# A hybrid decoder layer: SBUF places, mix, key, query and V-row transfers of the attention stage rearranged

## The chip, the cores and the metric

One Trainium2 chip, one core, float32. The metric is the device time of one execution in microseconds (us), the median of the runs. The engines are TensorE (PE, with its weight loads as PEld), VectorE (DVE), ScalarE (ACT), GpSimd (POOL) and SyncE (SP). Every engine works through its own instructions in order. DMA transfers are issued by SP, ACT and POOL, each of which has a queue of its own.

## What is computed

One layer for a prompt of 4096 tokens and for 64 sample tokens (8 sequences of 8), width 1024:

```python
h = _rmsnorm(x, g_pre)
z = h @ w_in                      # 1024 -> 2816 columns, split into
cb, cc, ch, cg, q, k, v, ag, mq, mg = _split_cols(z)
out_a = silu(cg) * cb * conv3(cc * ch)                    # 256 columns
out_b = silu(ag) * window_attention(q, k, v, sink)        # 512 columns, window 128, 8 heads on 2 kv heads
out_c = silu(mg) * cross_attention(mq, mem_k, mem_v)      # 256 columns, 256 memory tokens, 4 heads
y = concatenate([out_a, out_b, out_c]) @ w_out            # 1024 -> 1024
return x + _rmsnorm(y, g_post)
```

The keys and values of the window and of the memory and the ends of the convolution are returned as well.

## The kernel before

**Two stages.** The input projection runs in three phases over 8 blocks of 520 tokens each; phases 1 and 2 make every product from seven partial products (a Strassen scheme, `PRODUCTS`), and a step is one such product `p` of one block `b`. Phase 2 (`ph == 2`) projects six column tiles, the queries 10, 11 and 18 to 21. Its 56 steps are counted by `n = 7 * (b - 1) + p`, and `third_jobs` places other work into them: the keys and values of the memory, the turning of V into rows (`v_load`, `v_turn`), and the scores and weights of the first three attention groups (`EARLY`, `PIECES`). Results go to DRAM: `qd` (keys and queries, a high and a low part), `vd` and `vn` (V as columns and as rows), `md` (the gates, called mix).

The attention stage then runs over 32 blocks of 128 tokens (`blocks`, `Block.run`); in the course of block `i`, `events_of(i, block)` calls for the work on other groups at fixed places `(p, k)` between the matmuls of the output projection (half `p` of the columns, row tile `k`; line 1617 in the profile). In block `i` group `i + 3` gets its scores (`scores`: band scores `ws`, cross scores `xs`), group `i + 1` its values (`values`: products `pv`, then the gate on DVE, lines 1336 and 1367, which multiplies into the mix), and block `i + 1` is split for the output projection (`split`, `mh` and `ml`). A chunk is two groups: 256 tokens, whose keys `kst` (384 KB), queries `q` (two halves of 768 KB) and mix (1 MB) are loaded together for the two.

**The way of a group's weights.** After the softmax (`s`) DVE turns the weights in blocks of 32 x 32 (`turn(0, g)`, `turn(1, g)`; lines 1303 and 1307), 16 transfers of 64 KB move them to `w` (line 1312; by SP, for the first three groups by POOL), POOL masks the bands (`turn(2, g)`, line 1322, four instructions into `wd` and `w`), and then the values of the group can be multiplied.

**Order.** From the start of phase 2 on, the order on each engine is the order in which the code is written. `store` appends its transfer to a list `late` that `flush` sends to SP's queue at the start of a step and after every product. SP's transfers before the steady blocks are: the `qd` stores of the projection's last rows, `blocks[0].load()` and `blocks[1].load()` (`xr`, 512 KB each), the 16 of `w3`, the output `o_yp` of block 0, a V row tile `vh`, the next `xr`, the 16 of `w4`.

**Places.** SBUF places are stacks of pools, and the attention stage opens its pools (`open_attention`) where those of the projection ended. A tile waits until the pools that its own pool overlaps have had their last use. In bytes per partition, counted from the first place behind `place`:

| Phase 2 | before | after the change |
|---|---|---|
| `hx` (x tiles; at the end raw rows of `w_out`) | 0 to 16640 | the same |
| `hp` (high and low parts of x) | 16640 to 33280 | the same |
| `t2` (temporary tiles; at the end the high parts of six rows) | 33280 to 45760 | the same |
| `z8` / `z9` | 45760 / 49920 | 45760 / 52000 |
| `y0` / `y1` | 54080 / 56160 | 49920 / 56160 |
| `z10` / `y2` (to 64480) | 58240 / 62400 | the same |

In the last block of phase 2, the rows of the first half lie in `z9` and `y1`, those of the second in `z10` and `y2`; `z8` and `y0` were last used by the block before.

| Attention stage | before | on | after the change | on |
|---|---|---|---|---|
| `yq` (products times gain) | 0 | `hx` | 0 | `hx` |
| `kp` (keys of even chunks) | 28928 | `hp` | 4096 | `hx` |
| `mixp` (mix of odd chunks) | 8448 | `hx` | 7168 | `hx` |
| `bq` (queries of even chunks) | 16640 | `hp` | 16640 | `hp` |
| `sp` (scores of even groups from 4) | 32000 | `hp`, `t2` | 45760 | `z8`, `y0`, `z9` |
| `wl` (turned weights of odd groups from 3) | 40192 | `t2`, `z8` | 53952 | `z9`, `y1`, `z10` |
| `yp` (two `xr`) | 48384 | `z8`, `z9`, `y0`, `y1` | 35072 | `t2` |
| `wd0`, `wd1` (masked halves) | 4096, 6144 | `hx` | 43264, 62144 | `t2`; `z10`, `y2` |
| `sm`, `bp` (sample) | 56576, 57344 | `y1`; `y1`, `z10`, `y2` | 15360, 28928 | `hx`; `hp`, `t2` |

The mix of even chunks lies in `place`, the queries and keys of odd chunks and the weights of even groups elsewhere; these do not move.

Of the kernel before, what the change touches and what calls it, by code (L numbers as in the profile page):

```python
# [8 lines left out]
F32 = mybir.dt.float32  # L9
# [6 lines left out]
P = 128  # L16
# [4 lines left out]
NS = 64  # L21
# [5 lines left out]
NCH = 4096 // CT  # L27
# [24 lines left out]
def hybrid_layer(ctx: ExitStack, tc: tile.TileContext, a: dict):  # L52
    nc = tc.nc
    DMA = nc.sync
# [67 lines left out]
    def z_pool(where, name, w=2):  # L122
        return where.enter_context(tc.tile_pool(name=name, bufs=1))

    def open_phase(ph):
        nonlocal tp, natp, pa2, pa1

        if ph == 0:
            z = [z_pool(kept_z, f"z{n}") for n in range(4)]
            natp = own.enter_context(tc.tile_pool(name="nat", bufs=2))  # L130
            zp[2] = [*z, z_pool(own, "z4")]
            kept_z.z4 = zp[2][-1]
        elif ph == 1:
            zp[2].remove(kept_z.z4)
            zp[2][:0] = [z_pool(own, f"z{n}") for n in (5, 6, 7)]
        else:
            tp = own.enter_context(tc.tile_pool(name="t2", bufs=6))
            z = [z_pool(own, n) for n in ("z8", "z9", "y0", "y1", "z10", "y2")]
            zp[2], zp[1] = [z[0], z[1], z[4]], [z[2], z[3], z[5]]
        if ph < 2:  # L140
            tp = own.enter_context(tc.tile_pool(name=f"t{ph}", bufs=(7, 9)[ph]))
        bank = lambda where, name, bufs=1: where.enter_context(tc.tile_pool(name=name, bufs=bufs, space=bass.MemoryType.PSUM))
        if ph == 0:
            pa2 = {(tag, 0): bank(psa, f"p{tag}2") for tag in "yx"} | {(tag, 1): bank(own_banks, f"p{tag}3") for tag in "yx"}
        elif ph == 2:
            own_banks.close()
            third["ps"] = bank(psa, "psm", 2)
            pa1 = {("y", 2): pa2["y", 0], ("x", 2): pa2["x", 0], ("x", 1): bank(psa, "px1"), ("y", 1): bank(psa, "py1")}
# [22 lines left out]
            zp[w] += [used[w][i] for i in order if i < len(used[w])]  # L171
            used[w] = []

    late = []

    def flush():
        for fn in late:
            fn()
        late.clear()

    store_queue = [G]

    def store(dst, src):
        if store_queue[0] is G:
            G.dma_start(dst, src)
        else:
            late.append(lambda: DMA.dma_start(dst, src))
# [554 lines left out]
    third = {}  # L742
# [120 lines left out]
    def open_group(g):  # L863
# [6 lines left out]
              (4, 0, of("early_cross_exps")), (4, 1, of("band_weights")), (5, 0, of("early_cross_weights")), (5, 0, of("turn_band")),  # L870
              (6, 0, of("turn_cross")))
    PIECES = {0: (*STAGES, (9, 0, of("masks")), (15, 0, of("values"))), 1: (*STAGES, (9, 0, of("masks")), (15, 0, of("values"))),
              2: (*STAGES, (11, 2, of("masks")))}

    def v_load(k):
        third["v", k] = t = temp(f"vl{k}")[:, :512]
# [2 lines left out]
    def v_turn(k):  # L879

        turned = temp(f"vq{k}")[:, :512]
        V.transpose(turned, third.pop(("v", k)))
        rows_of = vn[512 * k : 512 * k + 512, :].rearrange("(b i) d -> i b d", i=32)
        for g in range(4):
            ds = slice(32 * g, 32 * g + 32)
            store(rows_of[:, :, ds], turned[ds].rearrange("p (b j) -> p b j", j=32))

    def first_chunk():

# [74 lines left out]
    def input_projection():  # L964
        for i, (ph, b, p) in enumerate(steps):
# [39 lines left out]
                slots[0].append(gpost_load)  # L1005
            if ph == 2 and b == last:
                for n, j in enumerate(((), (), (), (0, 1, 2, 3), (4, 5, 6, 7), (8, 9, 10, 11), (12, 13, 14, 15))[p]):
                    slots[(0, 0, 2, 2)[n] if p == 6 else (0, 1, 1, 2)[n]].append(lambda j=j: wo_split(j))
                for j in ((), (0, 2, 4), (6, 8), (), (10, 12, 14), (), ())[p]:
                    slots[2].append(lambda j=j: wo_load(j))  # L1010
                if p == 6:
                    slots[0].insert(0, blocks[0].split)
# [45 lines left out]
    def open_attention():  # L1058

        nonlocal ps, mixp, wp, wl, kp, bp, bq, yp, yq, sp  # L1060
        own.close()
        psa.close()
        pa.close()

        ps = {tag: ctx.enter_context(tc.tile_pool(name=f"ps{tag}", bufs=1, space=bass.MemoryType.PSUM)) for tag in (*range(4), "pv", 4, 5)}
        left = lambda name, bufs=1: att.enter_context(tc.tile_pool(name=name, bufs=bufs))
        yq, wd0, wd1 = left("yq"), left("wd0"), left("wd1")
        left("gap").tile([P, NS], F32, name="gap")
        mixp, bq, kp, sp, wl, yp = left("mixp"), left("bq"), left("kp"), left("sp"), left("wl"), left("yp", 2)
        wp = wd0, wd1  # L1070
        third["sm"], bp = left("sm"), left("bp")

    ps = mixp = wp = wl = vp = kp = bp = bq = yp = yq = sp = None
    att = ctx.enter_context(ExitStack())
# [36 lines left out]
    class Chunk:  # L1111
# [25 lines left out]
        def load_mix(self):  # L1137

            if self.c % 2 == 0:
                self.mix = place.rearrange("p a k n -> p (a k n)")[:, : KT * CT].rearrange("p (k n) -> p k n", k=KT)  # L1140
            else:
                self.mix = mixp.tile([P, KT, CT], F32, tag="mix", name=f"mix{self.c}")
            (G if 0 < self.c < 3 else DMA).dma_start(self.mix, md[:, :, self.ts].rearrange("k p n -> p k n"))

        def early_values(self):

# [16 lines left out]
    class Group:  # L1163
# [32 lines left out]
        def scores(self):  # L1196
            self.open_scores()
            bands = [psum(n, f"ws{self.b}_{n}").rearrange("p (h k) -> p h k", h=2) for n in ((1, 2, 5, 4) if self.b == 4 else range(4))]
            cross_bank = lambda hh: psum(hh if self.b == 4 else 4 + hh, f"xs{self.b}_{hh}").rearrange("p (j k) -> p j k", j=2)
            if self.b != 4:  # L1200
                cross = [cross_bank(hh) for hh in range(2)]
            self.bands(bands[:2], 0)
            tail(0)
            self.bands(bands[2:], 1)
            if self.b == 4:
                cross = [cross_bank(hh) for hh in range(2)]
            self.crosses(cross)
            if self.b == 4:
                turn(1, 3)
            loads = query_loads((self.b - 3) // 2 + 3) if self.b % 2 and self.b > 3 else ()  # L1210
            for fn in loads[:2]:
                fn()
            tail(1)
            for fn in loads[2:]:
                fn()
            if self.b == 3:
                blocks[1].split(0)
            self.band_softmax()
            return cross
# [190 lines left out]
    def query_loads(c):  # L1410
        if c >= NCH:
            return ()
        chunks[c] = Chunk(c)
        return [chunks[c].load_keys, lambda: chunks[c].load_queries(0), lambda: chunks[c].load_queries(1)]

    def chunk_load(c):
# [257 lines left out]
    def events_of(i, block):  # L1674
# [3 lines left out]
        def at(p, k, fn, *args):  # L1678
            ev.setdefault((p, k), []).append(lambda: fn(*args))
# [11 lines left out]
        if i == 30:  # L1691
            at(0, 5, blocks[32].split)
            at(1, 1, blocks[31].split)
            at(1, 6, blocks[31].load)
        if i % 2 == 0:
            if i == 28:
                at(0, 3, lambda: chunks[15].load_mix())
        elif 1 < i and (i + 3) // 2 < NCH - 1:
            at(0, 3, lambda: chunks[(i + 3) // 2].load_mix())
        at(1, 1, turn, 2, i + 2)  # L1700
        if i == 0:
            at(1, 1, chunk_load, 3)
        if i == 1:
            at(1, 1, lambda: chunks[2].load_mix())
        if i > 0 and i + 3 < 2 * NCH:
            at(0, 5, half_load, i + 3)
        if i > 1:
# [126 lines left out]
```

## Time and profile before

| | |
|---|---|
| median of 3 runs | 1494.75 us (1494.41 to 1496.84) |
| profiled execution | 1492.81 us, its span 1491.1 us |
| granted TensorE clock, mean | 0.996 |
| PE / DVE / ACT / POOL busy | 1463.1 / 1212.2 / 758.0 / 457.5 us |
| phase 2, first to last product | 668.22 to 942.05 us |
| output projection starts | 942.05 us |
| moved by DMA | 337.27 MB, mean 226 GB/s |

The span counts from the first to the last instruction; the time has the start and the end of the execution around it. In a row of the timeline stand: start, duration (us), engine, line, operation, tiles written <- tiles read, count, and in square brackets how long the engine had idled before and what it waited for. Tile names in the profile are without their number: `s` is any of `s3`, `s4`. Where rows of one instruction follow each other they are merged, and the duration is that of all.

### The profile page before, as it was taken

Reading aid. Unit: us, or ns where it says so; the run is one execution under the profiler, and the core shown is the slowest. Engines: PE = TensorE matmul, PEld = TensorE weight load, DVE = VectorE, ACT = ScalarE, POOL = GpSimd, SP = SyncE. Lnnn points to the kernel's source line nnn. Section 1 sums busy time; section 2 is a strip of 40 time slices with the busy share of each in tenths; the row PEclk is TensorE's granted clock in tenths of the full one; section 3 lists DMA queues with packets and bytes.
Section 4 is the critical chain, followed back from the end, with each engine's and each line's share of the span. In section 5 each row is a group of like instructions: output and inputs, shape, how many; then the busy total and the mean of one; then the engine's idle time right before and its main releaser. Section 6 shows DMA issues by size and latency. Waiting matters only on the chain.

```text
span 1491.1 us, 30884 instructions
## 1 busy us (share of the span) xinstructions
PE 1463.1 (98%) x11459; PEld 1339.4 (90%) x11459; DVE 1212.2 (81%) x1889; ACT 758.0 (51%) x1869; POOL 457.5 (31%) x633
## 2 busy tenths in 40 slices
PE   9999999999999999999999999889999999999998
PEld 9999999999999999999999999767777777777766
DVE  6779888898998877797667877878988888898853
ACT  6776566466422222244544454555655655565542
POOL 0223332212300000000002225445566465565551
PEclk9999999999999999999999999999999999999999
DMA  9989999887854333258978989998999998989672
GB/s 256 193 244 229 289 289 275 230 272 247 233 208 161 133 117 130 104 211 242 323 258 238 310 260 301 312 209 204 226 242 223 236 240 209 212 220 243 202 218 100
DMA packets 211068, 337.27 MB, mean 226 GB/s; under 512 B 55269, under 2 KB 124773, under 8 KB 210885
## 3 DMA queue, kind: packets, MB, share of 16 engines
q1 hardware_dynamic: 157429, 223.80, 51.1%
q0 software_dynamic: 44416, 79.73, 21.6%
q10 hardware_dynamic: 9072, 31.77, 6.9%
q8 instruction: 91, 1.49, 0.5%
q14 instruction: 60, 0.49, 0.1%
HBM read 192.48 MB, written 110.15 MB: 203 GB/s over the span
## 4 chain that ended last, share of the span: by engine, by line
PE 69%; DMA 13%; DVE 7%; issue 5%; SPq 4%; ACT 2%; POOL 1%; ACTq 0%; DVEq 0%; POOLq 0%
PE c L381 46%; PE y L1617 15%; DMA w<-s 4%; PE pv L1097 4%; SPq L1312 3%; PE ws L1097 1%; DMA qd<-z 1%; DMA mix<-md 1%; DMA place<-md 1%; DVE z L388 1%; DMA wor<-in_w_out 1%; DMA xr<-in_x_p 1%; PE mem_acc L809 1%; DMA o_yp<-xr 1%; PE xs L1097 1%
## 5 line engine op out<-in xcount | busy, mean ns | idle before, releaser
L1617 PE MATMUL y<-wo,mh 128*128 128x512 f32 (+1 forms) x1040 | 328.6, 391 | 0.0
L388 DVE TENSOR_TENSOR z<-c,z 128x520 f32<-128x520 f32 (+1 forms) x308 | 193.7, 643 | 79.0 <-PE c L381 72.6
L1617 PEld LDWEIGHTS y<-wo,mh 128*128 128x128 f32 x1040 | 194.2, 188 | 52.5 <-DVE wmx L1255 5.4
L1617 PE MATMUL y<-wo,ml 128*128 128x512 f32 (+1 forms) x520 | 201.1, 387 | 0.0
L1295 POOL TENSOR_SCALAR s<-s,xrd 128x256 f32<-128x256 f32 x128 | 60.8, 489 | 209.2 <-DVE xrd L1292 163.0
L1617 PEld LDWEIGHTS y<-wo,ml 128*128 128x128 f32 x520 | 97.8, 188 | 18.7 <-DVE ml L1592 0.2
L1265 ACT ACTIVATE s<-s,wnm 128x128 f32<-128x128 f32 x256 | 98.7, 387 | 0.0
L1242 ACT COPY s<-ws 128x256 f32<-128x256 f32 x128 | 41.1, 378 | 90.9 <-PE ws L1097 65.2
L754 POOL MEMSET negs<- 128x1 f32 x1 | 0.1, 98 | 267.2 <-PE c L381 267.2
L1647 POOL TENSOR_TENSOR xr<-yn,xr 128x1024 f32<-128x1024 f32 x31 | 74.4, 2399 | 24.2 <-ACT yn L1646 24.0
L1625 ACT ACTIVATE y<-y 128x512 f32<-128x512 f32 (+1 forms) x66 | 38.6, 584 | 62.5 <-DVE yn L1624 54.1
L1322 POOL TENSOR_SCALAR_AFFINE_SELECT wd<-w 128x512 f32<-128x512 f32 x64 | 54.4, 850 | 42.1 <-DMA w<-s 29.4
L1246 DVE COPY_PREDICATED s<-wmask,ws 128x256 f32<-128x256 uint8 x124 | 47.9, 438 | 20.1 <-ACT s L1242 13.0
L1624 DVE TENSOR_TENSOR yn<-y,gpost 128x512 f32<-128x512 f32 (+1 forms) x66 | 44.7, 678 | 17.7 <-PE y L1617 16.7
L1322 POOL TENSOR_SCALAR_AFFINE_SELECT w<-w 128x512 f32<-128x512 f32 x64 | 58.3, 929 | 2.2
L1097 PEld LDWEIGHTS ws<-kst,q 64*128 64x128 f32 x768 | 47.7, 185 | 11.9 <-issue 9.9
L1288 ACT ACTIVATE s<-xs,xnm 128x256 f32<-128x256 f32 x128 | 57.9, 459 | 0.0
L1097 PE MATMUL ws<-kst,q 64*128 64x256 f32 x768 | 55.0, 288 | 0.8 <-DVE z L388 0.8
L390 ACT COPY z<-c 128x520 f32<-128x520 f32 (+1 forms) x44 | 24.2, 554 | 54.9 <-PE c L381 51.6
L1646 ACT ACTIVATE yn<-yn,yst 128x1024 f32<-128x1024 f32 x31 | 35.7, 1150 | 28.0 <-POOL yst L1638 28.0
L1265 ACT ACTIVATION_READ_ACCUMULATOR s<-s,wnm 128x1 f32 x256 | 47.9, 187 | 0.0
L294 ACT ACTIVATE nat<-nat 104x1024 f32<-104x1024 f32 x40 | 42.2, 1055 | 9.0 <-DMA nat<-in_x_p 9.0
(957 smaller groups left out, 4983.2 us busy)
## 6 DMA issues: line engine op xcount, KB each, us to landing
w<-s SPq DMA_DIRECT2D x456, 64.0 KB
q<-qd POOLq DMA_DIRECT2D x32, 768.0 KB, 8.8
xr<-in_x_p SPq DMA_DIRECT2D x32, 512.0 KB
nat<-in_x_p SPq DMA_DIRECT2D x39, 416.0 KB
o_yp<-xr SPq DMA_DIRECT2D x31, 512.0 KB
md<-th POOLq DMA_DIRECT2D x48, 260.0 KB, 6.0
qd<-zh SPq DMA_DIRECT2D x48, 260.0 KB
qd<-z SPq DMA_DIRECT2D x48, 260.0 KB
```

The lines of the kernel that those rows point to most:

```text
L381: TE.matmul(bank[:, :HW], l, r, start=first and i == 0, stop=last and i == 3 * KH - 1)
L388: add = lambda dst, other: V.tensor_tensor(dst, c, other, op=ALU.add)
L1097: ins = TE.matmul(o, w, x, **kw)
L1246: V.copy_predicated(to, squares(third["wmask"]), squares(s3[:, :, 0:P]))
L1265: S.activation(sm[:, h], sm[:, h], AF.Exp, bias=nm[:, h : h + 1], scale=SCALE, accum_out=den[:, h : h + 1])
L1288: S.activation(p[:, i], s[:, i].rearrange("p (a k j) -> p a k j", a=2, k=4), AF.Exp, bias=nm[:, i : i + 1], scale=SCALE, accum_out=den[:, ...
L1295: G.tensor_scalar(p[:, i], p[:, i], rd[:, i : i + 1], 0.5, op0=ALU.mult, op1=ALU.mult)
L1312: (G if b < 3 or b == 31 and k % 2 else DMA).dma_start(to[32 * k : 32 * k + 32, g], self.squares[32 * g : 32 * g + 32, k])
L1322: G.affine_select(out, src, pattern=[[32 * sign, 2], [0, 8], [sign, 32]], compare_op=op, fill=0.0, base=base * sign, channel_multiplier=-s ...
L1617: TE.matmul(acc, self.hl[l][:, k], wo[k][c0 // 512][:, r, c0 % 512 : c0 % 512 + c1 - c0], start=j == 0, stop=j == passes * KT - 1)
L1624: V.tensor_tensor(yn[:m, c0:c1], acc[:m], gpost[0][:m, c0:c1], op=ALU.mult)
L1647: total = G.tensor_tensor(self.xr, yn, self.xr, op=ALU.add)
```

## The change

Six edits:

- In phase 2 `z9` and `y0` change places, and the attention stage's pools are laid in another order (tables above).
- The four stores of a V row tile (`vn`) are no longer sent together at the next `flush`: each `flush` sends one of them, after the other late stores.
- The masks of group 2 come at step `n = 44` (first slot) instead of `n = 45` (third slot). Splits 12 and 13 of `w_out` come after the second product of the last step instead of the first.
- The keys of a chunk are loaded in one block (odd group `b`, as before), both halves of its queries in the next (even `b`).
- The mix of chunk `c` from 3 to 14 is loaded in block `2c - 2` instead of `2c - 3`.
- The mix of chunk 2 is issued by SP instead of POOL, and in block 1 at `(0, 4)`, behind the scores, instead of `(1, 1)`.

```diff
-            z = [z_pool(own, n) for n in ("z8", "z9", "y0", "y1", "z10", "y2")]
-            zp[2], zp[1] = [z[0], z[1], z[4]], [z[2], z[3], z[5]]
+            z = {n: z_pool(own, n) for n in ("z8", "y0", "z9", "y1", "z10", "y2")}
+            zp[2], zp[1] = [z[n] for n in ("z8", "z9", "z10")], [z[n] for n in ("y0", "y1", "y2")]
...
-    late = []
+    late, late_rows = [], []
     def flush():
         for fn in late:
             fn()
         late.clear()
+        if late_rows:
+            late_rows.pop(0)()
...
-              2: (*STAGES, (11, 2, of("masks")))}
+              2: (*STAGES, (10, 0, of("masks")))}
...
-            store(rows_of[:, :, ds], turned[ds].rearrange("p (b j) -> p b j", j=32))
+            late_rows.append(lambda ds=ds: DMA.dma_start(rows_of[:, :, ds], turned[ds].rearrange("p (b j) -> p b j", j=32)))
...
-                    slots[(0, 0, 2, 2)[n] if p == 6 else (0, 1, 1, 2)[n]].append(lambda j=j: wo_split(j))
+                    slots[(1, 1, 2, 2)[n] if p == 6 else (0, 1, 1, 2)[n]].append(lambda j=j: wo_split(j))
...
-        yq, wd0, wd1 = left("yq"), left("wd0"), left("wd1")
-        left("gap").tile([P, NS], F32, name="gap")
-        mixp, bq, kp, sp, wl, yp = left("mixp"), left("bq"), left("kp"), left("sp"), left("wl"), left("yp", 2)
+        yq, kp, mixp, third["sm"] = left("yq"), left("kp"), left("mixp"), left("sm")
+        left("gap0").tile([P, 128], F32, name="gap0")
+        bq, bp, yp, wd0 = left("bq"), left("bp"), left("yp", 2), left("wd0")
+        left("gap1").tile([P, 112], F32, name="gap1")
+        sp, wl, wd1 = left("sp"), left("wl"), left("wd1")
         wp = wd0, wd1
-        third["sm"], bp = left("sm"), left("bp")
...
-            (G if 0 < self.c < 3 else DMA).dma_start(self.mix, md[:, :, self.ts].rearrange("k p n -> p k n"))
+            (G if self.c == 1 else DMA).dma_start(self.mix, md[:, :, self.ts].rearrange("k p n -> p k n"))
...
-            loads = query_loads((self.b - 3) // 2 + 3) if self.b % 2 and self.b > 3 else ()
-            for fn in loads[:2]:
+            loads = query_loads(self.b // 2 + 2)[:1] if self.b % 2 and self.b > 3 else query_loads(self.b // 2 + 1)[1:] if self.b > 4 else ()
+            for fn in loads[:1]:
                 fn()
             tail(1)
-            for fn in loads[2:]:
+            for fn in loads[1:]:
                 fn()
...
-        chunks[c] = Chunk(c)
+        if c not in chunks:
+            chunks[c] = Chunk(c)
...
-        if i % 2 == 0:
-            if i == 28:
-                at(0, 3, lambda: chunks[15].load_mix())
-        elif 1 < i and (i + 3) // 2 < NCH - 1:
-            at(0, 3, lambda: chunks[(i + 3) // 2].load_mix())
+        if i % 2 == 0 and 2 < i < 2 * NCH - 2:
+            at(0, 3, lambda: chunks[i // 2 + 1].load_mix())
...
         if i == 1:
-            at(1, 1, lambda: chunks[2].load_mix())
+            at(0, 4, lambda: chunks[2].load_mix())
```

## The prediction

> **What bounds the kernel now.** I read the page first: the span, and the engines' busy shares.
>
> ```profile
> span 1491.1 us, 30884 instructions
> PE 1463.1 (98%) x11459; PEld 1339.4 (90%) x11459; DVE 1212.2 (81%) x1889; ACT 758.0 (51%) x1869; POOL 457.5 (31%) x633
> ```
>
> TensorE is busy for 1463.1 of 1491.1 us, so a change that keeps every matmul can move little more than 28 us, and none of its edits touches a matmul. So I asked next what the matmuls waited for, from 690 us, early in the third phase of the projection, to the end. Columns: in all, times, longest.
>
> ```profile
> PE xs L1097 <- DVE s L1246: 4.3, 1, 4.3
> PE pv L1097 <- DMA w<-s: 4.2, 1, 4.2
> PE pv L1097 <- ACT y L1625: 3.4, 8, 0.9
> PE c L381 <- DVE lo_7T L372: 1.4, 1, 1.4
> ...
> PE c L381 <- DVE lo_4T L372: 1.0, 1, 1.0
> PE pv L1097 <- DMA vh<-vn: 1.0, 1, 1.0
> PE ws L1097 <- DVE z L388: 0.8, 1, 0.8
> ```
>
> Two waits stand out, one each. The table of stages (PE, PEld, DVE, ACT, POOL busy, then granted clock, DMA share, GB/s) places the first right behind the projection, and shows that the clock falls there too; a later stretch of 100 us loses 0.8 us of PE.
>
> ```profile
> 960.00:980.00 20.00, 15.74 (x102) 11.85 (x98) 11.48 (x23) 9.00 (x33) 7.99 (x10) 0.83 0.93 242
> ...
> 1060.00:1160.00 100.00, 99.23 (x711) 78.49 (x709) 88.77 (x157) 60.41 (x222) 56.74 (x70) 1.00 0.95 227
> ```
>
> Then the timelines of the two places, PE's and ACT's first: group 4's band scores ran at 959.40, but ACT could not copy them into `s4` until 964.46, when a store `qd<-zh` of the projection's last rows had landed, and the cross scores stood for 4.26 us. `s4` lies on the pools `t2` and `hp`; the last of their six stores frees it.
>
> ```profile
> 959.40 1.69 PE L1097 MATMUL ws<-kst,q 64*128 64x256 f32 x24
> ...
> 965.47 1.65 PE L1097 MATMUL xs<-mk,q 64*128 64x256 f32 x11 [4.26 <-DVE s L1246]
> 964.46 1.20 ACT L1242 COPY s<-ws 128x256 f32<-128x256 f32 x4 [4.93 <-DMA qd<-zh]
> ```
>
> The chain of waits (start, us) gives what the lower clock costs: a `pv` product took 4.54 and 3.99 us right after the two waits, 2.48 undisturbed; `xs` took 1.65 (above) against 0.72.
>
> ```profile
> 967.12 4.54 PE pv L1097 x32
> ...
> 1002.54 3.99 PE pv L1097 x32
> ...
> 1019.26 0.72 PE xs L1097 x12
> 1019.97 2.48 PE pv L1097 x32
> ```
>
> So the first wait is worth 4.26 + 2.06 + 0.93 = 7.25 us, the second 4.2 + 1.51 = 5.7. These 13 us are the ground on which the change plays.
>
> **Part by part: the places.** `sp` moves onto `z8`, `y0` and `z9`, all freed by the first half of the last rows. When? The `xr` loads of before lie on `z8`, `z9`, `y0`, `y1`, and SP issued them at 958.60, so these were free by then.
>
> ```profile
> 958.60 0.83 SPq L1572 DMA_DIRECT2D xr<-in_x_p  x2
> 967.69 11.21 SPq L1312 DMA_DIRECT2D w<-s  x16
> 979.00 0.53 SPq L1650 DMA_DIRECT2D o_yp<-xr  x1
> ...
> 981.98 0.33 SPq L1572 DMA_DIRECT2D xr<-in_x_p  x1
> 983.11 13.05 SPq L1312 DMA_DIRECT2D w<-s  x16
> ```
>
> ACT's wait goes: -4.26, and the slow stretch with it, -2.99. But `kp` moves from `hp` onto `hx`, where `w_out`'s raw rows lie. What a place on `hx` waits for is seen in `mix<-md` of before, which lies there: for the last split of `wo` on DVE.
>
> ```profile
> 943.37 0.73 POOL L1129 DMA_DIRECT2D kst<-qd  x1
> ...
> 946.00 0.82 POOL L1135 DMA_DIRECT2D q<-qd  x1 [1.03 <-issue]
> 947.89 0.89 POOL L1143 DMA_DIRECT2D mix<-md  x1 [1.06 <-DVE wo L204]
> ```
> ```profile
> 946.07 1.27 DVE L204 TENSOR_TENSOR wo<-wor,wo 128x512 fp32r<-128x512 f32 x2
> ```
> ```profile
> q<-qd POOLq DMA_DIRECT2D x1, 768.0 KB, 13.1
> ```
>
> So `kst2`, and behind it on POOL both halves of chunk 2's queries and the mix, start up to 947.34 - 943.37 = 3.97 us later. The second half was issued at 946.00 and took 13.1 us (the last row, KB and us to landing): it landed at 959.1, and PE used it at 959.40. There is no slack. Bounds of the delay: 0 (SP's stores have the DMA engines to themselves meanwhile, and the bytes until 959 are the same) and 3.97. I take 2.0, the middle, since both ends are real: band scores at 961.1, +1.7. At the end of group 2's values: -4.26 - 2.99 + 1.7 = -5.55 (bounds -7.25, and -0.6 if the delay is whole and the clock falls again).
>
> The clock's part hangs on how long the new wait is: 4.26 us brought the slow stretch, the 1.4 us for `lo_7T` did not. [...]
>
> Next on this path is `w3`, the turned weights of group 3: transposes, 16 transfers by SP, masks by POOL, values.
>
> ```profile
> 964.97 0.77 DVE L1246 COPY_PREDICATED s<-wmask,ws 128x256 f32<-128x256 uint8 x2 [5.07 <-DMA xr<-in_x_p]
> ...
> 966.42 1.24 DVE L1307 STREAM_TRANSPOSE s<-s 128x1024 f32<-128x1024 f32 x1
> ```
> ```profile
> 1146.86 1.69 PE L1097 MATMUL ws<-kst,q 64*128 64x256 f32 x24
> ```
> ```profile
> 1148.28 0.78 DVE L1246 COPY_PREDICATED s<-wmask,ws 128x256 f32<-128x256 uint8 x2 [0.62 <-ACT s L1242]
> ...
> 1169.39 0.42 DVE L1336 TENSOR_TENSOR mix<-mix,pv 128x256 f32<-128x256 f32 x1 [0.46 <-PE pv L1097]
> ```
> ```profile
> 980.45 1.52 POOL L1322 TENSOR_SCALAR_AFFINE_SELECT wd<-w 128x512 f32<-128x512 f32 x2 [0.31 <-DMA w<-s]
> ...
> 983.39 0.99 POOL L1143 DMA_DIRECT2D place<-md  x1
> ...
> 1001.22 1.52 POOL L1322 TENSOR_SCALAR_AFFINE_SELECT wd<-w 128x512 f32<-128x512 f32 x2 [7.64 <-DMA w<-s]
> ```
>
> The transposes stand behind group 4's copies on DVE. In a quiet block the copies start 1.4 us after the band scores (1146.86, 1148.28), so here at 962.5 instead of 964.97, and the transposes 2.5 us earlier than 966.42. And `xr` moves onto `t2`: SP, in order, now stands at `xr` until the last `qd<-zh` has landed (964.46, as ACT's row shows), so `w3` can start at 964.46 + 0.83 = 965.3, 2.4 before 967.69. Its masks began 0.31 us after a wait in before, without PE waiting, so they were just in time; now they are 2.4 earlier while PE is 5.55 earlier: a new wait of about 3.1 in front of group 3's masked values, and the gain there is -2.4. I keep 0 and -5.5 as bounds.
>
> **Chunk 2's mix, and keys and queries apart.** `w4` started at 983.11 and was ready at 1001.22, 18.1 us later; `w3` took 980.45 - 967.69 = 12.8. Beside `w4` POOL's queue moved the mix (983.39) and, right behind it, chunk 4's keys and both halves of its queries: 2.9 MB. After the change only the keys (0.38 MB) are left there; the mix is issued by SP behind `w3`, four transfers before `w4`. `w4` starts 2.4 earlier (its `xr` waits for `o_yp`, 979.00 to 981.98, both shifted): 980.7. Bounds of its time: 12.8 and 18.1; I take 13.5, near `w3`'s, which also ran beside 2 MB of another queue: ready at 994.2. PE comes there at 1002.54 - 4.2 - 2.4 = 995.9, so the wait and its slow stretch go: -5.7, in all -8.1.
>
> **The mix a block later, in the steady blocks.** The mix of an odd block went out just before that block's 16 `w`, and these took 15.22 us instead of 10.58; that late `w` is what PE waited for at 1166 (the 1.0 above, put down to the last transfer of the queue).
>
> ```profile
> 1130.62 10.58 SPq L1312 DMA_DIRECT2D w<-s  x16
> ...
> 1142.42 0.38 SPq L1143 DMA_DIRECT2D mix<-md  x1
> ...
> 1144.68 15.22 SPq L1312 DMA_DIRECT2D w<-s  x16
> ```
> ```profile
> 1207.57 9.13 DMA mix<-md
> ```
>
> With keys in one block, queries in the next and the mix beside the keys, the bytes of two neighbours come closer. I take -1.0 (the 1.0), bounds 0 and -3 (with most of the eight waits for ACT). The queries, loaded a block later, are first used two blocks after that; 13.1 us fit into one block of 16, so they cost nothing; without that block they would cost what they lack. Keys and queries stand on POOL before the residual add and the cross weights as before, with two issues fewer in one block and two more in the next.
>
> **The rest**: V's rows one store per product, masks of group 2 1.7 steps earlier, two splits of `wo` a product later. SP doesn't wait for products, so most rows go out when they did. These act on the waits of 1.4, 1.0 and 0.8: bounds -3.2 and +1.4. I take nothing, because chunk 2's queries, not PE, set when group 4's scores start, so 2.2 of it is hidden there. The sample's stages keep their work; one mix comes beside their loads: nothing, at worst one wait like the 4.2.
>
> **Sum**: -8.1 - 1.0 = -9.1. The profiled execution took 1492.81 us (span 1491.1 and 1.7 around it), so 1483.7; the median of the runs is 1494.75, 1.94 above it: **1485.6**.
>
> **Rivals.**
> First, the queries of chunk 2 are late by the whole 3.97, and the clock falls again: -0.6, then the relief of `w4` -5.7 and -1.0: -7.3, 1487.5. For it: no slack at 959.1. Against: the engines catch up. 0.12.
> Second, `w4` stays late, since 1 MB of mix, 0.5 of `xr` and 0.5 of `o_yp` now go ahead of it in its own queue: only -2.4 - 1.0, 1491.3. [...] Against: the 1.5 MB of queries do leave. 0.13. Both together: -1.6, 1493.2, within the noise: 0.08.
> Third, the mix comes too late, and the kernel is slower. Its place on SP is behind a block's 16 `w`. If these start at 1144.68 and take 10.58, the mix goes out 1.2 later (as at 1142.42) at 1156.5 and lands at 1165.6 (9.13); the gate that needs it ran at 1169.39, or 1168.4 without PE's wait: 2.8 us of slack. If the `w` take 15.22 and the mix, beside queries, the 13.1 of a queries' half, it lands at 1174.2, 5.8 too late. DVE then stands in every second block; its idle 11% (88.77 of 100 busy) of the 32 us of two blocks takes up 3.6, and 2.2 are left, 12 times for the chunks 3 to 14: +26 on -8.1, 1512.7. It decides from 2.8 + 3.6 = 6.4 us of delay on. For it: SP's times swing by 4.6 us, and the queries now load just as the mix lands. Against: what made SP swing moves away. 0.17.
> The forecast keeps 0.50.
>
> So faster by over 0.2% (3 us, about what a measurement of this kernel can tell from no change): 0.50 + 0.12 + 0.13 = 0.75; the same 0.08; slower 0.17. The range reaches down to both stalls gone and -1 on top (-14, 1480.7) and up past the two rivals and their sum by this 0.2%, to 1496.0; it leaves out the third.
>
> **What would show it.** Right: no `qd<-zh` ahead of ACT's copy of `s4`; `kst<-qd` behind `wo`'s splits at 946 to 947; band scores of group 4 waiting 1 to 3 us for `q<-qd`; `xr` issued about 964; `w4` ready within 14 us; `w` of all later blocks near 11 us. Wrong: clock under 0.9 at 960 to 980, `place<-md` or `mix<-md` as what DVE L1336 waits for, or 18 us for `w4`.

## The result, and the profile after

| | before | after |
|---|---|---|
| median of 6 runs | 1494.58 us (1492.32 to 1496.84) | 1484.2 us (1479.19 to 1484.73) |
| ratio | | 0.9926, 95% interval 0.9910 to 0.9942 |
| profiled execution | 1492.81 us, span 1491.1 | 1484.73 us, span 1483.0 |

The change takes 10.4 us off the median, 8.1 off the profiled execution. The prediction said 1485.6 and 1483.7. The total was right; of its terms one was right, one was nothing, one was six times as large as forecast and for another reason.

The page of the changed kernel: PE is busy for 1461.4 us (1463.1 before), so 6.4 of the 8.1 us of the span are time in which it stood idle, and 1.7 are busy time.

```profile
PE 1461.4 (99%) x11459; PEld 1340.1 (90%) x11459; DVE 1205.1 (81%) x1889; ACT 757.5 (51%) x1869; POOL 456.9 (31%) x632
```

PE's waits after the change, from 690 us to the end (columns as before). The waits of 4.3 for `s` and of 4.2 for `w` are gone; two waits in front of `ws` and one in the sample are new.

```profile
PE ws L1100 <- DMA qd<-z: 2.9, 1, 2.9
...
PE sms L1457 <- DMA sq<-in_cmk: 2.0, 1, 2.0
...
PE ws L1100 <- DMA q<-qd: 1.3, 1, 1.3
```

The table of stages: the clock still falls at 960 to 980 (0.83 as before), and PE, which in the steady blocks at 1160 to 1260 was busy for 98.46 of 100 us before (first row), is now busy for all of them (last row).

```profile
1160.00:1260.00 100.00, 98.46 (x706) 77.61 (x705) 88.32 (x153) 59.57 (x213) 58.44 (x73) 1.00 0.92 229
```

```profile
960.00:980.00 20.00, 17.97 (x132) 14.85 (x134) 12.94 (x25) 9.09 (x33) 6.72 (x8) 0.83 0.93 235
...
1160.00:1260.00 100.00, 100.00 (x730) 78.93 (x725) 88.68 (x156) 59.21 (x214) 61.27 (x72) 1.00 0.91 232
```

The timelines behind the projection, PE's, POOL's and SP's. Chunk 2's keys go out at 946.45, behind the splits of `w_out`; PE stands at group 4's band scores for 2.93 us and, two matmuls later, for 1.33; the rest of `ws` takes 2.72 us, the first row of a slow stretch. The view puts the first of these waits down to a store `qd<-z`; by the trace's landing times it ended with the first half of chunk 2's queries (issued at 947.18, landed at 960.29), while the keys had landed at 952.17. `w4` starts at 983.38 and is masked at 996.15, 12.8 us later (18.1 before).

```profile
960.70 0.38 PE L1100 MATMUL ws<-kst,q 64*128 64x256 f32 x2 [2.93 <-DMA qd<-z]
962.41 2.72 PE L1100 MATMUL ws<-kst,q 64*128 64x256 f32 x22 [1.33 <-DMA q<-qd]
```
```profile
946.45 0.73 POOL L1132 DMA_DIRECT2D kst<-qd  x1 [3.24 <-DMA qd<-z]
...
980.73 1.52 POOL L1325 TENSOR_SCALAR_AFFINE_SELECT wd<-w 128x512 f32<-128x512 f32 x2 [2.28 <-DMA w<-s]
...
996.15 1.51 POOL L1325 TENSOR_SCALAR_AFFINE_SELECT wd<-w 128x512 f32<-128x512 f32 x2 [3.62 <-DMA w<-s]
```
```profile
959.05 0.81 SPq L1576 DMA_DIRECT2D xr<-in_x_p  x2
967.50 11.66 SPq L1315 DMA_DIRECT2D w<-s  x16
...
983.38 10.26 SPq L1315 DMA_DIRECT2D w<-s  x16
```

**Where the time went, stage by stage.** The starts of the same matmuls in the two traces, subtracted: group 3's band scores 945.25 and 943.55 (-1.7), group 3's values 982.30 and 981.97 (so 1.4 lost in between: 37.05 and 38.42 us), group 7's band scores 1017.56 and 1012.01 (5.2 won: 35.26 and 30.04), the sample's first scores 1400.82 and 1388.91 (6.4 won: 383.26 and 376.90), its last products 1452.42 and 1443.59 (3.1 lost: 51.60 and 54.68). The 1.7 at the start can't be told from the spread of single executions: in the twelve kernels below, those scores start between 943.2 and 953.5, in no order that follows the parts of the change. (The two latest are the two with the keys on `hp`; both profiled executions ran some 8 us above the median of their kernel.) That is why the table below reads distances, not times of day.

### The profile page after: what moved, and what is told of

It reads as the page before. It is cut to its first block, busy times and chain, and to the rows that moved or that the text cites. A ratio compares the mean times of both kernels' runs of the same rounds, so it can differ in the third digit from the quotient of the medians.

```text
span 1483.0 us, 30887 instructions
## 1 busy us (share of the span) xinstructions
PE 1461.4 (99%) x11459; PEld 1340.1 (90%) x11459; DVE 1205.1 (81%) x1889; ACT 757.5 (51%) x1869; POOL 456.9 (31%) x632
## 4 chain that ended last, share of the span: by engine, by line
PE 76%; DMA 10%; DVE 4%; issue 4%; SPq 2%; POOL 1%; ACT 1%; ACTq 0%; POOLq 0%; DVEq 0%
PE c L383 49%; PE y L1621 18%; PE pv L1100 4%; PE ws L1100 2%; SPq L1315 2%; DMA place<-md 1%; DMA wor<-in_w_out 1%; DMA w<-s 1%; PE xs L1100 1%; DMA q<-qd 1%; DMA qd<-z 1%; DMA sq<-in_cmk 1%; PE mem_acc L811 1%; DMA svm<-in_cmv 1%; DMA wr_0S<-sd10S 1%
## 5 line engine op out<-in xcount | busy, mean ns | idle before, releaser
L1629 ACT ACTIVATE y<-y 128x512 f32<-128x512 f32 (+1 forms) x66 | 38.7, 586 | 64.0 <-DVE yn L1628 54.3
L1100 PEld LDWEIGHTS ws<-kst,q 64*128 64x128 f32 x768 | 48.9, 189 | 15.5 <-issue 13.2
L1249 DVE COPY_PREDICATED s<-wmask,ws 128x256 f32<-128x256 uint8 x124 | 48.0, 441 | 16.4 <-ACT s L1245 13.2
```

The source lines that it names most:

```text
L1100: ins = TE.matmul(o, w, x, **kw)
L1249: V.copy_predicated(to, squares(third["wmask"]), squares(s3[:, :, 0:P]))
```

## The experiments

The ratio is that of a kernel to the kernel before on the same chip, with its 95% interval. Kernels with `p_` are the kernel before with parts of the change, those with `a_` or `b_` the changed kernel with an edit. "First blocks" is the distance from group 3's to group 7's band scores, "22 blocks" that from group 7's to group 29's (start of the PE rows `ws`), in the one profiled execution of each; a block without any wait took 15.95 us, so 22 of them take 350.9. "Ahead" is how many of a chunk's three loads POOL issues ahead of the residual add (`xr<-yn,xr`) of the same block (2 where any block has two).

| kernel | median us | ratio | first blocks | 22 blocks | ahead |
|---|---|---|---|---|---|
| before | 1494.58 | 1 | 72.31 | 357.86 | 2 |
| after | 1484.2 | 0.9926 (0.9910 to 0.9942) | 68.46 | 352.48 | 1 |
| `p_places` | 1495.0 | 1.0004 (0.9991 to 1.0016) | 74.02 | 358.63 | 2 |
| `p_sched` | 1486.12 | 0.9945 (0.9931 to 0.9958) | 67.53 | 353.15 | 1 |
| `p_qk` | 1485.57 | 0.9931 (0.9914 to 0.9948) | 67.19 | 353.09 | 1 |
| `p_q4` | 1491.29 | 0.9974 (0.9962 to 0.9986) | 67.91 | 359.29 | 2 |
| `p_q5` | 1495.66 | 1.0003 (0.9989 to 1.0016) | 72.19 | 357.47 | 2 |
| `a_mix_back` | 1483.56 | 0.9928 (0.9915 to 0.9941) | 69.97 | 353.64 | 1 |
| `a_qk_back` | 1489.72 | 0.9967 (0.9955 to 0.9980) | 70.73 | 355.61 | 2 |
| `a_rest_back` | 1484.41 | 0.9928 (0.9914 to 0.9941) | 69.63 | 351.84 | 1 |
| `a_kp_hp` | 1484.6 | 0.9935 (0.9913 to 0.9958) | 68.75 | 351.30 | 1 |
| `a_sample` | 1485.64 | 0.9935 (0.9918 to 0.9952) | 69.79 | 352.16 | 1 |
| `a_c3` | 1488.62 | 0.9954 (0.9938 to 0.9970) | 74.86 | 351.46 | 1 |
| `b_kp_c3` | 1486.35 | 0.9946 (0.9925 to 0.9966) | 69.76 | 352.25 | 1 |

**The places alone: `p_places`.** The kernel before with the first two pieces of the diff (the order of `z9` and `y0`, and the pools).

> The kernel before with the places alone (z9 and y0 exchanged, the attention pools laid anew), no other edit. By the prediction's sum: the first stall gives 2.4 us at group 3's values and block 4's late w keeps its 5.7 us, so about 1494.6 - 2.4 = 1492.2. By the trace of after: group 4's queries come 3.3 us late, the clock falls again, and at group 3's values only 0.3 us are won, so 1494.3, no difference; the granted clock at 960 to 980 is below 0.9, and the 4.2 us wait for w near 1002 is there.

No difference. PE's longest waits in it: the wait for the last `qd<-zh` has become one for chunk 2's queries (the 2.5 for `qd<-z`, by the landing times as above, and 1.2 more), the next is for group 3's `w` (2.4, put down to ACT; the way is shown at `a_kp_hp` below), and block 4's wait for `w` is still there (3.5 of the 4.5).

```profile
PE pv L1098 <- ACT y L1626: 5.6, 9, 2.4
PE pv L1098 <- DMA w<-s: 4.5, 2, 3.5
PE ws L1098 <- DMA qd<-z: 2.5, 1, 2.5
```

**The load schedule alone: `p_sched`.** The kernel before with the pieces of the diff from the mix's queue (`G if self.c == 1 else DMA`) to the end.

> The kernel before with the load schedule alone: the mix a block later, keys and queries in different blocks, the mix of chunk 2 by SP at (0, 4); places, V rows, masks and splits as before. By the prediction's sum: the first stall of 7.25 us stays, block 4's w comes in time (-5.7), the steady blocks give 1.0: 1494.6 - 6.7 = 1487.9. By the trace of after, where the steady blocks gave 6.4 us and the sample's wait took 3 back: -5.2 - 6.4 + 3 = -8.6, so 1486.0, nearly all of the change's gain. If the places are what frees the steady blocks as well, 1489 to 1491.

8.2 us of the 10.4, without any place moved. The first wait of 4.2 for `s` is still there and costs nothing against the other kernels: from group 3's band scores to its values this kernel takes 36.68 us, the changed one 38.42.

**Which part of the schedule: `a_mix_back`, `a_qk_back`.** The changed kernel with one part undone: the mix of chunks 3 to 14 again in block `2c - 3`; or keys and queries in one block again.

```diff
-        if i % 2 == 0 and 2 < i < 2 * NCH - 2:
-            at(0, 3, lambda: chunks[i // 2 + 1].load_mix())
+        if i % 2 == 0:
+            if i == 28:
+                at(0, 3, lambda: chunks[15].load_mix())
+        elif 1 < i and (i + 3) // 2 < NCH - 1:
+            at(0, 3, lambda: chunks[(i + 3) // 2].load_mix())
```

> The changed kernel with the mix of chunks 3 to 14 back in block 2c - 3; all else as changed. If the mix a block later is what freed the steady blocks (the prediction's reason, at a sixth of its size), the 6.4 us of 1035 to 1400 come back: 1484.2 + 6.4 = 1490.6, with 16 w of 15 us beside the mix in the odd blocks. If the split of keys and queries did it, 1484 to 1485. If the two share it, 1487.

> The changed kernel with keys and queries of a chunk loaded in one block again; all else as changed. If the relief of block 4's w came from the queries that left its side (the prediction's reason), its w takes about 18 us again and +5.2 to 5.7 us come back near 1000: 1489.6; if it came from the mix of chunk 2 that left POOL's queue, that wait stays away. If the split also made the steady gain of 6.4, 1496; if the mix a block later made it, 1484 or 1489.6 by what block 4 does.

The mix a block later is worth nothing that the medians can tell (1483.56 and 1484.2); in the one profiled execution the 22 blocks differ by 1.2 us. The split of keys and queries is worth 5.5 us: without it the steady blocks go back to 355.61 (357.86 in the kernel before), and `w4` takes longer again, 982.08 to 998.57, 16.5 us:

```profile
982.08 12.54 SPq L1315 DMA_DIRECT2D w<-s  x16
```
```profile
998.57 1.52 POOL L1325 TENSOR_SCALAR_AFFINE_SELECT wd<-w 128x512 f32<-128x512 f32 x2 [6.94 <-DMA o_yp<-xr]
```

The 18.1 of before thus have two parts: chunk 4's queries (16.5 to 12.8: 3.7) and chunk 2's mix, which left POOL's queue (18.1 to 16.5: 1.6). `p_qk` below, which has the split but leaves this mix with POOL, gives the same two parts the other way round: its `w4` takes 14.5 us from its start to its masks, 3.6 less than before and 1.7 more than the change.

**The split alone, and its two halves: `p_qk`, `p_q4`, `p_q5`.** The kernel before with only the split; with it for chunk 4 alone; with it for the chunks from 5 on. The last two differ from the first in one more thing: both halves of the queries are issued ahead of the residual add (`loads[:2]`), in `p_qk`, as in the change, one ahead of it and one behind (`loads[:1]`).

```diff
             (p_q4)
+            if self.b in (5, 6):
+                loads = query_loads(4)[:1] if self.b == 5 else query_loads(4)[1:]
...
             (p_q5)
+            loads = query_loads(self.b // 2 + 2) if self.b % 2 and self.b > 3 else ()
+            if self.b > 6:
+                loads = loads[:1] if self.b % 2 else query_loads(self.b // 2 + 1)[1:]
...
             (p_qk: the loads of the change, and)
-            for fn in loads[:2]:
+            for fn in loads[:1]:
                 fn()
             tail(1)
-            for fn in loads[2:]:
+            for fn in loads[1:]:
                 fn()
```

> The kernel before with keys and queries of a chunk in different blocks, and nothing else. If the split alone frees the steady blocks (22 blocks of 1018 to 1375 stand 7.0 us over their floor of 15.95 us; 2.7 with the mix put back) and most of block 4's w: -4 steady, -4 at block 4: 1487. If split and later mix are needed together, 1491 or more. By the prediction's terms (split without price in the steady blocks, 3.7 of the relief at block 4): 1490.

> The kernel before with the queries of chunk 4 alone loaded a block after its keys; every later chunk as before. If the queries beside w4 cause the wait of 4.2 us near 1002 and the slow stretch behind it, both go and nothing else changes: about 4.6 us less (what the full split showed there), 1490; the 22 blocks after it keep their 7 us over the floor. If the gain of the split is only in the steady blocks, 1494.5.

> The kernel before with the split for the chunks from 5 on, chunk 4 as before: the complement of the other. If the steady blocks are freed by it, their excess over the floor falls from 7 to 2 or 3 us, block 4 still waits 4.2 us for w: 1490. If the split matters only at block 4, 1494.5.

`p_qk` has nearly all of the gain: this one part of the change does what the whole does, within the intervals. `p_q4` gives block 4's part, 3.9 us by its ratio (0.0026 x 1494.6; 2.1 to 5.7 by its interval), with the steady blocks as before. But `p_q5`, which loads the queries of all other chunks a block later just as `p_qk` does, gives nothing, and its blocks stay at 357.47. Of the 10.3 us of `p_qk` (0.0069 x 1494.6; 7.8 to 12.9) 3.9 are block 4's, and the other 6.4 don't come from the bytes that left the block. What `p_q5` does not share with `p_qk` is the place of the second issue on POOL.

The timelines of one chunk's block and the block after it show how this reaches PE, first in the kernel before (POOL, DVE, ACT, PE). The block starts with its band scores at 1180.35, the next at 1196.30.

```profile
1183.44 0.80 POOL L1129 DMA_DIRECT2D kst<-qd  x1
1184.25 0.84 POOL L1135 DMA_DIRECT2D q<-qd  x1
1185.10 2.40 POOL L1647 TENSOR_TENSOR xr<-yn,xr 128x1024 f32<-128x1024 f32 x1
```
```profile
1184.97 2.57 DVE L1256 SCALAR_TENSOR_TENSOR wnm<-wmx,nsink 128x8 f32<-128x8 f32 x1
...
1196.20 1.18 DVE L1592 TENSOR_TENSOR ml<-mix,mh 128x1024 fp32r<-128x1024 f32 x1
```
```profile
1187.78 0.21 ACT L1263 ACTIVATE wes<-wes 128x8 f32<-128x8 f32 x1 [3.11 <-DVE wes L1257]
...
1198.08 0.58 ACT L1625 ACTIVATE y<-y 128x512 f32<-128x512 f32 x1
```
```profile
1196.30 1.69 PE L1097 MATMUL ws<-kst,q 64*128 64x256 f32 x24
1198.82 1.09 PE L1097 MATMUL pv<-w,mv 128*64 128x128 f32 x16
```

And in the changed kernel, the block that loads queries and the one after it; they start at 1188.69 and 1204.64.

```profile
1191.81 0.91 POOL L1138 DMA_DIRECT2D q<-qd  x1
1193.12 2.39 POOL L1651 TENSOR_TENSOR xr<-yn,xr 128x1024 f32<-128x1024 f32 x1 [0.40 <-ACT yn L1650]
```
```profile
1193.31 2.23 DVE L1259 SCALAR_TENSOR_TENSOR wnm<-wmx,nsink 128x8 f32<-128x8 f32 x1
...
1204.19 1.18 DVE L1596 TENSOR_TENSOR ml<-place,mh 128x1024 fp32r<-128x1024 f32 x1
```
```profile
1195.77 0.21 ACT L1266 ACTIVATE wes<-wes 128x8 f32<-128x8 f32 x1 [2.74 <-DVE wes L1260]
...
1206.18 0.61 ACT L1629 ACTIVATE y<-y 128x512 f32<-128x512 f32 x1
```
```profile
1204.64 1.69 PE L1100 MATMUL ws<-kst,q 64*128 64x256 f32 x24
1206.98 1.09 PE L1100 MATMUL pv<-w,mv 128*64 128x128 f32 x16
```

With two issues ahead, POOL starts the add 4.75 us after the band scores, with one 4.43. DVE's `wnm`, an operation on 8 columns, does not end before the add does (1187.54 and 1187.50; 1195.54 and 1195.51). So ACT's exponentials of the group begin 7.43 and 7.08 us after the band scores, 0.35 apart, and most of this distance is handed on: DVE's split `ml` starts 0.10 and 0.45 us ahead of the next block's band scores, ACT begins its last reading of `y` 1.78 and 1.54 behind them, and the values, which need the bank that `y` lay in, start 2.52 and 2.34 behind them. That is 0.18 of PE's loss; another 0.15 comes within the values, where `pv<-w,vh` waits for POOL's masks of `w` (1.12 us from its start to the start of the next product, 0.97 in the changed kernel). The next block is 16.28 long in the kernel before (1196.30 to 1212.58) and 15.95 in the changed one (1204.64 to 1220.59). That happens to every second block: 11 times 0.33 are 3.6 of the 5.4 us between 357.86 and 352.48. The rest was not followed up; these second blocks take 16.29 to 17.54 us in the kernel before. `p_q5` has the same with two halves of queries, there with `wes`, the next small operation:

```profile
1265.12 1.75 POOL L1135 DMA_DIRECT2D q<-qd  x2
1266.88 2.42 POOL L1650 TENSOR_TENSOR xr<-yn,xr 128x1024 f32<-128x1024 f32 x1
```
```profile
1266.61 2.72 DVE L1259 TENSOR_TENSOR wes<-wnm,sink 128x8 f32<-128x8 f32 x1
```

Over all fourteen kernels the column "ahead" sorts the 22 blocks: 355.61 to 359.29 with two, 351.30 to 353.64 with one. It isn't the number of issues as such that counts, but whether the small operations run into the add: in the changed kernel's other blocks, which load keys, there is also one issue ahead, yet the add starts later, 5.40 us behind the band scores, because it waits for ACT's `yn`; `wnm` is through before it (at 1209.26, in 0.17 us), and the exponentials begin as early as 5.21 behind. That DVE waits for the add is read from the coinciding ends. That the order on POOL is the cause rests on `p_q5` against `p_qk`, which differ in one more thing, chunk 4's loads, and `p_qk` sends the second half's bytes one add later, too. A version with all issues behind the add was not run.

**The passage behind the projection: `a_kp_hp`, `a_c3`, `b_kp_c3`.** Since the places gave nothing, three tries to get their gain after all: the keys of even chunks back on `hp` (so that they needn't wait for `w_out`'s rows); chunk 3's 1.9 MB issued in block 1 instead of block 0; both.

```diff
-        yq, kp, mixp, third["sm"] = left("yq"), left("kp"), left("mixp"), left("sm")
-        left("gap0").tile([P, 128], F32, name="gap0")
-        bq, bp, yp, wd0 = left("bq"), left("bp"), left("yp", 2), left("wd0")
-        left("gap1").tile([P, 112], F32, name="gap1")
-        sp, wl, wd1 = left("sp"), left("wl"), left("wd1")
+        yq, mixp, wd0, wd1 = left("yq"), left("mixp"), left("wd0"), left("wd1")
+        left("gap0").tile([P, NS], F32, name="gap0")
+        bq, kp, third["sm"], bp, yp = left("bq"), left("kp"), left("sm"), left("bp"), left("yp", 2)
+        sp, wl = left("sp"), left("wl")
```
```diff
-        if i == 0:
-            at(1, 1, chunk_load, 3)
         if i > 0 and i + 3 < 2 * NCH:
             at(0, 5, half_load, i + 3)
+        if i == 1:
+            at(0, 5, chunk_load, 3)
```

> The changed kernel with the keys of even chunks back on hp, behind the queries; to make room both masked halves lie on hx, the sample's tiles and xr move up by at most 4 KB, the scores of even groups still on z8, y0, z9. If chunk 2's keys stood in front of its queries because of w_out's rows on hx (the prediction's second step), they now go out 3 us earlier, about 943, the queries land by 959, the wait of 4.3 us in front of group 4's band scores shrinks to about 1 and the clock at 960 to 980 stays at 1.0: 2 to 5 us less than the change, 1479 to 1482. If the queries are late for another reason (the DMA engines are full with the projection's last stores), the wait stays, 1484.

> The changed kernel with chunk 3's keys and queries issued in block 1, behind the first residual add on POOL, instead of block 0: 1.9 MB leave 958 to 970, where the DMA engines are full, for 968 on, where half of them idle (share 0.48). If the passage behind the projection is bound by the DMA engines, the projection's last stores, the queries of chunk 2 and w3 come earlier, group 3's values start 2 to 3 us sooner and the clock stays up: 1479 to 1481. If w3 then shares with the 1.9 MB instead, its 16 transfers take 15 us instead of 12, or block 4's w 18 instead of 13: 1486 to 1490.

> The changed kernel with both: keys of even chunks on hp, and chunk 3's loads in block 1. If the passage behind the projection is bound by the DMA engines, the keys going out earlier no longer delay the projection's last stores, xr and w3, and this is the fastest: 1477 to 1480. If only the order of the transfers matters and w3 is held as before, 1484.

None is faster than the change. In `a_kp_hp` the first half of the guess holds: the keys go out 1.3 us ahead of group 3's band scores (952.18, the scores at 953.46) instead of 2.9 behind them, the wait in front of group 4's shrinks to 0.92, and the clock at 960 to 980 is 1.00. (Its profiled execution lost 8 us in the projection, before any of this, so only distances are read.) But now group 3's values wait, 5.15 us, and the clock falls there:

```profile
969.00 1.58 PE L1099 MATMUL ws<-kst,q 64*128 64x256 f32 x22 [0.92 <-DMA q<-qd]
...
990.11 1.97 PE L1099 MATMUL pv<-w,mv 128*64 128x128 f32 x16 [5.15 <-ACT y L1628]
```
```profile
960.00:980.00 20.00, 18.98 (x129) 14.94 (x128) 15.03 (x32) 14.32 (x58) 5.61 (x9) 1.00 1.19 364
980.00:1000.00 20.00, 14.85 (x101) 11.19 (x100) 14.28 (x31) 9.31 (x38) 11.34 (x14) 0.83 0.82 213
```

Those values wait for `w3`: SP issued `xr` at 971.95 and the 16 transfers behind it from 973.15 on. The chain of waits (start, us) has the last store `qd<-zh` in flight ahead of that and `xr` behind it. From `w3`'s landing (988.71) the way to the values leads over ACT, which only then copies scores into `s` and after that reads `y`; hence the view's name for the wait:

```profile
961.43 10.39 DMA qd<-zh
...
972.34 9.38 DMA xr<-in_x_p
...
986.72 1.99 DMA w<-s
...
989.45 0.61 ACT y L1628 x2
```

`a_c3` shows the other side: with chunk 3's bytes gone the DMA engines' share at 960 to 970 fell from 1.39 to 0.55 (the changed kernel's row, then `a_c3`'s; the share counts the time of all packets, and so can be above 1), and chunk 2's second half of queries was in flight for 12.13 us instead of 12.37, no sooner there; but `w3`, now beside the 1.9 MB, came late (17.6 us from its start to its masks, 13.2 in the changed kernel), and group 3's values waited 5.68 us.

```profile
960.00:970.00 10.00, 7.97 (x69) 6.55 (x70) 4.91 (x9) 2.74 (x7) 3.92 (x4) 0.66 1.39 362
```
```profile
960.00:970.00 10.00, 7.95 (x69) 6.54 (x70) 5.03 (x10) 2.84 (x7) 3.59 (x3) 0.66 0.55 193
```

```profile
962.32 2.71 PE L1100 MATMUL ws<-kst,q 64*128 64x256 f32 x22 [2.05 <-DMA q<-qd]
...
986.22 1.98 PE L1100 MATMUL pv<-w,mv 128*64 128x128 f32 x16 [5.68 <-ACT y L1629]
```

So chunk 3's bytes don't hold the queries back. Whether other traffic does stays open: chunk 3's loads are issued from 958.58 on in the changed kernel, when the queries have been in flight for 8 us and more, and the share at 955 to 960 is 1.24 there and 1.28 in `a_c3`. What holds is narrower: from group 3's band scores to its values, every kernel but `a_c3` takes 36.0 to 38.7 us, whichever wait stands in between, and the masks of `w3` start 34.7 to 37.4 us behind those scores, one to two before the values. That `w3` sets this stretch is read from these distances, from the chain above and from `a_c3`, where both came late together; no edit that speeds `w3` up was run. `b_kp_c3`, with both edits, lies in the same range (37.85 us, a wait of 5.7 in front of the values) and gains nothing either.

**The rest: `a_rest_back`, `a_sample`.** V's rows, masks of group 2 and the two splits as before; and the sample's second memory keys issued ahead of chunk 15's mix.

```diff
-            at(0, 3, lambda: chunks[i // 2 + 1].load_mix())
+            at(0, 3 if i < 28 else 4, lambda: chunks[i // 2 + 1].load_mix())
...
-              (28, 0, 4): mem1, (28, 1, 4): mem1, ...
+              (28, 0, 3): mem1, (28, 1, 4): mem1, ...
```

> The changed kernel with V's rows stored four at a time, the masks of group 2 and the splits 12 and 13 of w_out where they were. The prediction took them at nothing, since chunk 2's queries set when group 4's scores start: 1484.2. The trace of after shows the projection's end 1.7 us earlier; if that is theirs and is not eaten by the wait for the queries, 1485.9. If V's rows also set the waits of the later phase 2, 1487.

> The changed kernel with the sample's second half of memory keys issued ahead of the mix of chunk 15 instead of behind it. If the wait of 2.0 us in front of the sample's scores, and the slow stretch of 1 us behind it, come from the 1 MB of mix in front, both go: 1481.2. If the mix of chunk 15 then comes too late for the gate of group 30, no gain, 1484 or more.

Neither moves the median. In `a_sample` the wait of 2.0 for `sq` is gone from the list, but two others of 1.1 and 0.9 stand in the same stage:

```profile
PE y L1621 <- ACT y L1629: 1.1, 1, 1.1
PE smt L1429 <- DVE sq L1464: 0.9, 1, 0.9
```

## Why the prediction was right, and where it was not

- **The places, -2.4: wrong, 0** by the medians of `p_places`, and in the changed kernel's profile 1.4 us lost between group 3's scores and its values. ACT's wait for the last `qd<-zh` did go. The step that failed is the size of chunk 2's delay: taken as 2.0 between bounds of 0 and 3.97, it was 3.3 (the second half, below, landed at 962.37 instead of 959.1), and PE had come 1.6 earlier, so the wait was 2.93 + 1.33 and the clock fell again, to the 0.83 that the prediction had named as a sign of being wrong. Why the transfer of the queries takes 12 to 13 us there stays open. This is the first rival's mechanism, which had a chance of 0.12 (0.20 with the sum of both). The next step fell with it: `w3` was not 2.4 earlier. `xr` went out at 959.05, even before the 964.46 I had read from ACT's row, but the transposes stood behind group 4's copies, and those behind the late scores: the masks came at 980.73 (980.45 before). The clock's part: that a wait of 1.7 us would leave the clock up (the -2.99 in the sum) and one of 3.7 would not (the first rival) were my estimates between the 1.4 and the 4.26 us of the trace of before. No run has these very waits; in `b_kp_c3` one of 1.66 us (at 969.48) left the rest of `ws` at 1.56 us, and in `p_qk` one of 3.87 (at 965.56) was followed by an `xs` of 1.65, as in the kernel before. The chain of waits of the changed kernel has the path: `w_out`'s last two splits on DVE, then POOL, then the queries.

```profile
944.71 1.22 DVE wo L206 x2
...
950.00 12.37 DMA q<-qd
```

- **Block 4's `w`, -5.7: right,** -5.2, and for the reason given: it was ready 12.8 us after its start (13.5 forecast). `p_q4` and `a_qk_back` show chunk 4's queries as the larger part.
- **The steady blocks, -1.0: wrong in size and cause,** -6.4 in the profiles, beyond the bound of -3. The mix a block later had been given that 1.0, and it is worth 0 to 1.2. The step that failed is "keys and queries stand on POOL before the residual add and the cross weights as before, with two issues fewer in one block and two more in the next", priced at nothing. The order that it names isn't that of the change: before, the keys and the first half stood ahead of the add and the second half behind it; after, one load stands ahead of it in each block. I looked at the bytes and at the time until first use, not at what POOL does next and who waits for that. The trace of before had it: every second block 16.3 long or longer, with the add ending when `wnm` does.
- **The rest, 0: right** (`a_rest_back`). **The sample, 0: the profile lost 3.1,** within the "one wait like the 4.2" given as the worst. Most of it belongs to this one execution: from the sample's first scores to its last products `p_sched`, `a_rest_back`, `a_kp_hp`, `a_c3` and `b_kp_c3`, which have the same loads there, take 51.9 to 52.6 us, against 54.7 here and 51.6 before.
- **Second and third rival:** `w4` did not stay late, and no mix came too late; nowhere from 1000 us on does DVE's gate wait for a transfer of the mix.
- **The sum:** +1.4 - 5.2 - 6.4 + 3.1 = -7.1, with -1.7 at the start and +0.7 at the very end the 8.1 of the profile. The forecast of -9.1 was near it by luck: what the places lacked (2.4 not won and 1.4 lost) and the sample's loss (3.1) were for the most part made up by a gain that had not been seen (5.4).

## What to carry to other kernels

A transfer's issue is an instruction of its engine (on POOL 0.80 and 0.84 us for the two ahead of the add at 1185.10): before a load is moved, look at what stands behind it in that queue and at who waits for that, not only at its bytes. When a wait is removed, follow the stretch to the next thing that all ways through it share (here `w3`), since that may set the time whichever wait stands in front. Blocks of a steady loop that alternate by a third of a microsecond are worth a look at their start, not at their busy shares.

## What the runs showed of the hardware

**A tiny DVE operation lasted until POOL's add was through.** `wnm` on 128x8 took 2.57 and 2.23 us in the rows above, beside POOL's adds of 2.40 and 2.39, ending within 0.04 us of them; where it is through before the add begins, it takes 0.17, as in `p_q5` ahead of the stretched `wes` (the row below). Over the fourteen traces `wnm` or `wes` overlaps an add 293 times: 251 of them end 0.02 to 0.04 us behind the add, the other 42 within 0.15 us of its start; all that overlap none take 0.17.

```profile
1266.41 0.17 DVE L1258 SCALAR_TENSOR_TENSOR wnm<-wmx,nsink 128x8 f32<-128x8 f32 x1
```

What holds the small operation is not in the rows: by the stamps `wnm` started 0.13 us before the add in the first case (1184.97 and 1185.10) and lasted until its end all the same (1187.54 and 1187.50).

**In these traces the clock falls by the idle time in windows of 3.41 us, not by the length of one wait.** In `a_mix_back` two waits of 1.45 and 1.59 us with two matmuls in between left the clock of 960 to 980 at 1.00, and the rest of `ws` took 1.58 us:

```profile
960.03 0.38 PE L1100 MATMUL ws<-kst,q 64*128 64x256 f32 x2 [1.45 <-DMA qd<-z]
962.00 1.58 PE L1100 MATMUL ws<-kst,q 64*128 64x256 f32 x22 [1.59 <-DMA q<-qd]
```

In the changed kernel 2.93 and 1.33 brought it to 0.83 and the same matmuls to 2.72, like the single wait of 4.26 in the kernel before. But no limit for a wait, nor for the sum of two, comes out of the runs: a single wait of 2.73 us (`a_qk_back`, at 960.42) brought the clock of 960 to 980 to 0.91, and one of 3.19 (`p_q4`, at 969.61) left it at 1.00. The traces' records of the granted clock tell why. In the attention stage its slow stretches, at 0.50, last 3.41 or 6.83 us, and within one execution their starts lie whole multiples of 3.41 us apart (in the kernel before 964.56 and 1002.11, eleven times as far). In the 3.41 us ahead of such a start PE was idle for 3.03 us in the changed kernel and for 2.73 in `a_qk_back`, whose wait falls into one such window; the 3.19 of `p_q4` are split over two, 1.79 and 1.40, and so are those of `a_mix_back`, with 1.63 and 1.51 us idle. Of all the windows at full clock in the fourteen traces, from 940 us to the end of the sample's products, the 22 in which PE was idle for 1.95 us or more were followed by a slow one, and none of the others, with 1.79 or less (in the kernel before 3.36 and 3.41, the next 0.86; in the changed one 3.03 and 1.95, the next 1.30).
